# Seven products for the gate pair of layer two, with one of them run first, and a forget gate on column groups

## The chip, the cores and the metric

The kernel runs on one core of one Trainium2 chip. Times are device microseconds of one execution; the time of a version is the median of its runs. The engines meant below are TensorE (PE, and PEld for its weight loads), VectorE (DVE), ScalarE (ACT), GpSimd (POOL) and SyncE (SP), which here issues most DMAs.

## What is computed

Two layers of a streaming encoder, for 512 tokens of 2048 features, all in fp32. The parts that matter here:

```python
def hybrid_layer(x, w_in, w_out, g_pre, g_post, w_alpha, b_alpha, g_gla, g_att, rel_bias):
    h = rmsnorm(x, g_pre)
    z = h @ w_in
    gq, gk, gv, gg, ga, aq, ak, av, ag = split_columns(z)
    log_a = jax.nn.log_sigmoid((ga @ w_alpha + b_alpha).astype(jnp.float32)) / GLA_TAU
    o_gla = gla_chunk_causal(gq, gk, gv, log_a)
    ...
    o_gla = o_gla * jax.nn.silu(gg)
    o_att = chunk_band_attention(aq, ak, av, rel_bias)
    ...
    o_att = o_att * jax.nn.silu(ag)
    y = jnp.concatenate([o_gla, o_att], axis=-1) @ w_out
    return x + rmsnorm(y, g_post)
```

(Reshapes into heads are left out.) `ga`, the input of the forget gate, has only 16 columns. All else of `z` is 14 blocks of 512 columns: AG0 and AG1 (attention gate), AV0 and AV1, QK01 to QK67 (attention's queries and keys), GK and GQ, GV0 and GV1, GG0 and GG1. `w_out` is four more blocks, W01 and W23.

## The kernel before

**Products.** An fp32 product is made of three fp32r products: high times high, high times low, low times high, where the high part is a cast and the low part what the cast lost. Twelve matmuls of 128x512 (three terms, two halves of 256 input features, two token tiles) make a *job*: one block product for one of four chunks `c` of features. For the query and key blocks the result stands feature-major, and a job is 24 matmuls of 128x256.

A pair of blocks is multiplied for 512 tokens as a two-by-two scheme with seven block products P1 to P7 in place of eight (`fast_gemm`, L330): the input A is cut in token halves and feature halves (A11, A12, A21, A22), the weights in feature halves ("top", "bottom") and the two blocks. P1 uses A11 and P2 A12 directly, P4 uses A22, the others the sums S1 to S4 of the input, which `make_sums` (L554) writes to DRAM once for a layer. The right-hand factors are running sums of the four weight quarters in the tile H: P1 takes H itself, P5 and P6 add a quarter to it (L200), P7 subtracts (L202), P2 takes a raw quarter and then adds it to H (L222), after which P4 uses H. P3 uses the raw tile of P6. So a pair has 28 jobs, written in `PROD` as "10 11 50 12 ..." (product, chunk). Two accumulators X and Y of two PSUM banks each are used in turn; at the end of a product its result is copied out by ScalarE (L346) or combined by VectorE (L351) and handed to a consumer.

**Jobs and queues.** A job has a load (0.5 MB of weights by SP into a ring `raw` of five tiles or `H` of four, and the input's operand into `sa`, ring of four), a high part (ScalarE's cast into `wh`, four tiles, L206, with VectorE's running sum ahead of it) and a low part (VectorE into `wl`, three tiles, L216). While the matmuls of a job are issued, `ahead()` prepares loads five, high parts four and low parts three jobs ahead. Every engine's queue is served in order; the order on each is fixed when the program is built, by a scheduler that places instructions by estimated ready times. The rest (attention, the GLA recurrence, norms) are generator tasks, of which `pump` puts a few steps between jobs.

**The two layers.** Layer one multiplies AG0 and AG1 by a plain product (`std_gemm`, L299) while the input is prepared. Layer two does too, token half by token half, since the second half's tokens come later: 384 matmuls at L316. Then six pairs follow (`PAIRS`: AV, QKa, QKb, GK, GV, GG), then the out-projection (W01, W23) with an order of its own.

**The forget gate** (`forget_gate`, L751) multiplies the input's high and low parts by weights of 96 columns that hold the 16 gate columns split three times over in high and low parts: 64 matmuls of 128x256 a layer (L758), each keeping 96 of 128 columns of the array. `forget_gate_decay` (L773) multiplies its result, 98 rows, with `w_alpha` (L796, four matmuls a layer), all in fp32r.

**A22** is written to DRAM for P4 and loaded for each pair (`LEFT`, L185), 48 loads in all.

## Time and profile before

| what | us |
|---|---|
| median of 3 runs (lowest, highest) | 1615.64 (1615.36, 1617.37) |
| the profiled execution | 1613.77 |
| its span in the trace | 1611.8 |
| gate pair of layer two with its preparation (805.5 to 904.5) | 99.0 |
| six pairs of layer two (904.5 to 1448.3) | 543.8 |
| out-projection of layer two up to its last matmul (1448.3 to 1603.1) | 154.8 |

The stages' bounds are read from the first matmuls of each in the timeline. The profile is one execution; times in it count from the start of its span. "Busy" of TensorE overlaps, since a matmul's record lasts longer than the step to the next; steps are read from starts. An fp32 matmul appears as two records. A row of the groups names the line, the engine, the operation and the program's names, then busy time, mean duration and the idle time just before with what ended it. A row of the timeline has start, duration, and in brackets the idle time ahead. TensorE's granted clock is at full speed in all of the span. By stage, the columns being length, TensorE, its weight loads, VectorE, ScalarE and GpSimd, clock, DMA share and GB/s:

```profile
805.50:904.50 99.00, 98.85 (x483) 82.74 (x482) 80.63 (x109) 70.06 (x121) 21.61 (x40) 1.00 0.90 331
904.50:1448.30 543.80, 543.80 (x3293) 475.11 (x3292) 410.81 (x541) 297.01 (x503) 30.18 (x34) 1.00 0.75 259
1448.30:1603.10 154.80, 154.53 (x689) 127.27 (x687) 138.33 (x155) 90.08 (x132) 14.51 (x21) 1.00 0.78 268
```

### The profile page before, as it was taken

The numbers are of one execution on the slowest core, as the hardware profiler recorded it, in microseconds if no ns is written. First come the engines' busy times: TensorE is split into PE (matmuls) and PEld (weight loads), VectorE is DVE, ScalarE is ACT, GpSimd is POOL, SyncE is SP. The second block draws the span as 40 slices with busy tenths as digits, with TensorE's granted clock in tenths as the row PEclk, the third lists the DMA queues.
The fourth block names the chain that finished last, engine by engine and source line by source line (L and its number), as shares of the span: only waits on it lengthen the run. The fifth ranks groups of instructions, "written<-read, shape, count | busy, mean of one in ns | idle before, by whom it ended". The sixth has DMA issues, their size and how long they took to land.

```text
span 1611.8 us, 24496 instructions
## 1 busy us (share of the span) xinstructions
PE 1603.2 (99%) x8942; PEld 1373.1 (85%) x8942; DVE 1272.4 (79%) x1647; ACT 918.6 (57%) x1509; POOL 127.4 (8%) x192
## 2 busy tenths in 40 slices
PE   9999999999999999999999999999999999999998
PEld 7888999998888777888888889999988887788886
DVE  5977777678777877998988677786786778689887
ACT  7544445657455556665796444456675555465654
POOL 0120000010000000100122000000100000101001
PEclk9999999999999999999999999999999999999999
DMA  9797686685868768689779886867858687686887
GB/s 371 257 373 264 246 305 205 226 306 171 282 214 283 265 214 319 218 307 388 268 264 365 325 292 232 303 206 243 307 206 278 224 295 250 224 301 240 331 300 207
DMA packets 133928, 438.17 MB, mean 272 GB/s; under 512 B 14404, under 2 KB 27204, under 8 KB 133776
## 3 DMA queue, kind: packets, MB, share of 16 engines
q1 hardware_dynamic: 117360, 376.78, 66.9%
q0 software_dynamic: 16160, 59.53, 10.0%
q8 instruction: 71, 1.16, 0.3%
q14 instruction: 49, 0.40, 0.1%
q10 hardware_dynamic: 288, 0.30, 0.1%
HBM read 377.02 MB, written 61.62 MB: 272 GB/s over the span
## 4 chain that ended last, share of the span: by engine, by line
PE 95%; DVE 2%; DMA 1%; ACT 1%; issue 1%; SPq 0%; POOLq 0%; ACTq 0%; DVEq 0%
PE mm L394 54%; PE mm L384 19%; PE mm L316 10%; PE ax L951 2%; PE ax L394 2%; PE ax L1137 1%; PE ax L934 1%; PE ax L758 1%; PE ax L1109 1%; PE ax L914 1%; PE ax L913 1%; PE ax L912 1%; DVE wl L216 1%; DMA bias<-in_rel_dram 0%; PE ax L976 0%
## 5 line engine op out<-in xcount | busy, mean ns | idle before, releaser
L394 PE MATMUL mm<-wh,sa 128*128 128x512 f32 x1600 | 517.3, 394 | 0.5 <-ACT wh L206 0.5
L206 ACT CAST wh<-H 128x1024 fp32r<-128x1024 f32 x256 | 268.5, 1051 | 215.9 <-PE mm L394 96.1
L216 DVE TENSOR_TENSOR wl<-H,wh 128x1024 fp32r<-128x1024 f32 x256 | 311.9, 1220 | 93.3 <-PE mm L394 35.9
L394 PEld LDWEIGHTS mm<-wh,sa 128*128 128x128 f32 x1600 | 299.5, 188 | 72.3 <-issue 8.6
L206 ACT CAST wh<-raw 128x1024 fp32r<-128x1024 f32 (+1 forms) x233 | 243.9, 1051 | 204.4 <-PE mm L394 89.3
L216 DVE TENSOR_TENSOR wl<-raw,wh 128x1024 fp32r<-128x1024 f32 (+1 forms) x233 | 282.4, 1215 | 58.6 <-PE mm L394 23.5
L394 PE MATMUL mm<-wl,sa 128*128 128x512 f32 x800 | 312.7, 391 | 0.0
L384 PE MATMUL mm<-sa,wh 128*128 128x256 f32 x1280 | 237.4, 285 | 0.0
L394 PE MATMUL mm<-wh,a 128*128 128x512 f32 x640 | 211.5, 394 | 0.0
L384 PEld LDWEIGHTS mm<-sa,wh 128*128 128x128 f32 x1280 | 200.2, 191 | 0.3
L384 PE MATMUL mm<-sa,wl 128*128 128x256 f32 x640 | 181.0, 283 | 0.0
L394 PEld LDWEIGHTS mm<-wl,sa 128*128 128x128 f32 x800 | 150.3, 188 | 30.5 <-DVE wl L216 0.7
L200 DVE TENSOR_TENSOR H<-H,raw 128x1024 f32<-128x1024 f32 x144 | 174.8, 1218 | 1.0
L394 PEld LDWEIGHTS mm<-wh,a 128*128 128x128 f32 x640 | 119.5, 188 | 24.9
L394 PE MATMUL mm<-wl,a 128*128 128x512 f32 x320 | 125.7, 393 | 0.0
L384 PEld LDWEIGHTS mm<-sa,wl 128*128 128x128 f32 x640 | 122.5, 191 | 0.0
L436 POOL TENSOR_TENSOR sm<-sm,mhalf 128x2 f32<-128x2 f32 (+2 forms) x40 | 51.3, 1283 | 762.4 <-DVE sm L961 457.3
L202 DVE TENSOR_TENSOR raw<-H,raw 128x1024 f32<-128x1024 f32 x56 | 68.5, 1223 | 49.4 <-DMA raw<-in_w_dram 49.4
L394 PE MATMUL mm<-wh,g 128*128 128x512 f32 x320 | 101.5, 391 | 0.0
L384 PE MATMUL mm<-a,wh 128*128 128x256 f32 x512 | 95.4, 285 | 0.0
L346 ACT COPY ev<-mm 128x512 f32<-128x512 f32 x104 | 60.7, 584 | 60.0 <-PE mm L394 43.3
L222 DVE TENSOR_TENSOR H<-H,raw 128x1024 f32<-128x1024 f32 x48 | 58.7, 1223 | 38.0 <-DMA raw<-in_w_dram 37.7
(257 smaller groups left out, 2324.5 us busy)
## 6 DMA issues: line engine op xcount, KB each, us to landing
raw<-in_w_dram SPq DMA_DIRECT2D x311, 512.0 KB, 5.1
sa<-S SPq DMA_DIRECT2D x184, 512.0 KB, 4.5
H<-in_w_dram SPq DMA_DIRECT2D x64, 512.0 KB, 5.2
sa<-A SPq DMA_DIRECT2D x48, 512.0 KB, 6.2
S<-g POOLq DMA_DIRECT2D x32, 512.0 KB, 9.3
sa<-oS SPq DMA_DIRECT2D x32, 512.0 KB, 5.4
oS<-g POOLq DMA_DIRECT2D x16, 512.0 KB, 4.5
oS<-sa POOLq DMA_DIRECT2D x16, 512.0 KB, 5.7
```

Source lines behind the costliest of these rows:

```text
L200: nc.vector.tensor_tensor(out=h, in0=h, in1=r, op=ALU.add)
L202: nc.vector.tensor_tensor(out=r, in0=h, in1=r, op=ALU.subtract)
L206: last_cast[0] = nc.scalar.copy(self.wh[:, z, :], src[:, z, :]).ins
L216: last_low[0] = nc.vector.tensor_tensor(out=self.wl[:, z, :], in0=self.src[:, z, :], in1=self.wh[:, z, :].bitcast(F32), op=ALU.subtract).ins
L222: nc.vector.tensor_tensor(out=h, in0=h, in1=self.src, op=ALU.add)
L316: nc.tensor.matmul(pss[o], a(part, kk, o) if callable(a) else a[:, part, t], rhs[:, kk, :], start=(i == 0 and kk == 0 and m == 0), stop=(i ...
L346: last_copy[0] = nc.scalar.copy(e, src[t]).ins
L384: nc.tensor.matmul(dst, lhs[:, kk, f], a[:, part, tok], start=(fresh and kk == 0 and m == 0 and ft % 2 == 0), stop=(c == 3 and kk == 1 and ...
L394: last_mm[0] = nc.tensor.matmul(out_ps[t], a[:, part, tok], rhs[:, kk, :], start=(fresh and kk == 0 and m == 0), stop=(c == 3 and kk == 1 ...
L436: nc.gpsimd.tensor_tensor(out=out_r, in0=v, in1=mhalf[:, : v.shape[-1]], op=ALU.pow)
L758: nc.tensor.matmul(ps[0:96, half * 256 : (half + 1) * 256], wga[kt // 10][:, kt % 10, :], op[:, i, (kt % 2) * 256 : (kt % 2 + 1) * 256], s ...
L951: nc.tensor.matmul(o, self.pt[i][:, j * P : (j + 1) * P], av[hd // 4, j // 2][:, j % 2, (hd % 4) * P : (hd % 4 + 1) * P], start=(j == 0), ...
```

## The change

In layer two, AG becomes a pair of seven products like the others. `early_gemm` runs P2 (A12 times the first block's bottom quarter) of all seven pairs first, 28 jobs, as soon as the first token half is there; each result is copied out by ScalarE and written to DRAM by GpSimd's queue. The pairs then run `PROD_LATE`, 24 jobs. After P1 its copies get the early P2 added by two accumulating DMAs, and they are handed to the consumer after P4's job 1. With P2 gone from the pair, H lacks the bottom quarter, so P4 loads it again and adds it. P7's last job is ahead of P3's last; its combination is made at once, but in all pairs but AV its consumer runs only when P3 has ended. A22 is kept in four tiles for the layer. Layer one keeps `PROD`.

In both layers, the forget gate is computed by fp32 matmuls with 32 columns, on four column groups of the array by turns (the group `j` takes the feature block `2 kh + kk`), called once for each chunk inside `token_sums`, and the decay product is fp32 with 128 rows.

```diff
+    PROD_LATE = order("10 11 50 12 51 13 52 53 60 61 30 62 63 31 70 71 32 72 73 33 40 41 42 43")
...
-            elif k == "P2" or (k == "P4" and end):
+            elif k == "P2" or (k == "P4" and (end or late)):
                 p["r", self.c] = self.fetch(rtile("raw", bufs=5), b0, bottom)
...
+            if late and k == "P4":
+                if b0 == AG0:
+                    A[1, 1, c] = slot(f"a12{c}", [2, 512], F32R)
+                    nc.sync.dma_start(flat(A[1, 1, c]), src)
+                src = None
...
-                    if k in ("P5", "P6") or (k == "P4" and self.b0 >= NB_IN):
+                    if k in ("P5", "P6") or (k == "P4" and (self.b0 >= NB_IN or self.l)):
                         nc.vector.tensor_tensor(out=h, in0=h, in1=r, op=ALU.add)
...
-            stream += [Job(l, "std", c, b) for half in range(2) for b in (AG0, AG1) for c in CO]
+            stream += [Job(l, "std", 4 + c, b0) for b0, _ in (AG,) + PAIRS for c in range(4)]
...
+    def early_gemm(l, pair, rate):
+        acc = [ps_mm.tile([P, W], F32, tag="mm", name=nm("mm")) for _ in range(2)]
+        pace = Pace(rate)
+        for c in range(4):
+            job = take(l, pair[0], "std", 4 + c)
+            until(lambda: (1, 0, c) in A)
+            product(job, A[1, 0, c], acc, range(2), c == 0, c == 3, pair[0] in (QK01, QK45))
+            ahead()
+            pace()
+        for t in range(2):
+            e = ev()
+            last_copy[0] = nc.scalar.copy(e, acc[t]).ins
+            nc.gpsimd.dma_start(p2_d[pair][:, t, :], e)
...
-                consume(1, 1, t, None, combine(keep["p5"][t], src, ALU.subtract, keep["p5"][t]))
+                comb = combine(keep["p5"][t], src, ALU.subtract, keep["p5"][t])
+                if late and not direct:
+                    z = comb()
+                    held.append(lambda dst=None: z)
+                else:
+                    consume(1, 1, t, None, comb)
...
+            if late and (k, c) == ("P4", 1):
+                for t in range(2):
+                    finished("P2", t)
...
+                    if late:
+                        for t in range(2):
+                            nc.gpsimd.dma_start(keep["p1"][t], p2_d[pair][:, t, :], accum_op=ALU.add)
...
+                    if k == "P3":
+                        for t, comb in enumerate(held):
+                            consume(1, 1, t, None, comb)
...
+        def forget_gate(c):
+            if c == 0:
+                gate_ps.append(aux())
+            first = None
+            for half in (1, 0):
+                for j in (3, 2, 1, 0):
+                    kh, kk = divmod(j, 2)
+                    with tc.issue_after(first) if first else nullcontext():
+                        mm = nc.tensor.matmul(
+                            gate_ps[0][32 * j : 32 * (j + 1), half * 256 : (half + 1) * 256],
+                            fg_weights[l][:, 8 * kh + 2 * c + kk, :],
+                            full[half, c][:, kh, kk * 256 : (kk + 1) * 256],
+                            start=(c == 0 and half == 1), stop=(c == 3), skip_group_check=True,
+                        ).ins
...
         if l:
-            for half in range(2):
-                for q, b in enumerate((AG0, AG1)):
-                    std_gemm(
-                        l, b, (2 * half, 2 * half + 1), CO, operand_in, gate_evac(q), rate=1.3, lag=2 * half * q,
-                    )
-                if half == 0:
-                    tasks.append(token_sums(l))
-                    tasks.append(forget_gate())
+            tasks.append(token_sums(l, forget_gate))
+            for pair in (AG,) + PAIRS:
+                early_gemm(l, pair, 2.6)
+            fast_gemm(l, AG, gate_consume, rate=2.6)
...
-        fast_gemm(l, PAIRS[0], av_consume)
+        fast_gemm(l, PAIRS[0], av_consume, direct=True)
```

The function `product` holds the matmuls that stood in `fast_gemm` (L384, L394). Lines of the changed kernel differ: L200, L202 and L216 of before are L210, L212 and L226, L351 is L401, L316 is L326, L384 and L394 are L349 and L358.

The order of instructions changes with it. First VectorE in the pair AV of layer two, from the last subtraction for P7 on. Before (`L222` is P2's sum into H):

```order
L202 TENSOR_TENSOR raw_1795_9248<-H_1734_8951,raw_1795_9248 128x1024
L216 TENSOR_TENSOR wl_1788_9221<-raw_1766_9102,wh_1785_9203 128x1024
L202 TENSOR_TENSOR raw_1799_9269<-H_1744_8982,raw_1799_9269 128x1024
L216 TENSOR_TENSOR wl_1793_9244<-raw_1786_9205,wh_1789_9224 128x1024
L222 TENSOR_TENSOR H_1723_8879<-H_1723_8879,raw_1803_9290 128x1024
L216 TENSOR_TENSOR wl_1797_9264<-raw_1770_9123,wh_1794_9246 128x1024
L222 TENSOR_TENSOR H_1726_8897<-H_1726_8897,raw_1806_9308 128x1024
L216 TENSOR_TENSOR wl_1801_9285<-raw_1795_9248,wh_1798_9267 128x1024
L216 TENSOR_TENSOR wl_1804_9304<-raw_1799_9269,wh_1802_9288 128x1024
L351 TENSOR_TENSOR g0_1810_9329<-mm_1740_8963,ev_1791_9228 128x512
L222 TENSOR_TENSOR H_1734_8951<-H_1734_8951,raw_1813_9349 128x1024
L216 TENSOR_TENSOR wl_1807_9322<-raw_1803_9290,wh_1805_9306 128x1024
```

After (`L210` is now P4's sum into H; the last row is the low part of P4's job 0, the row two above it that of P3's job 3):

```order
L212 TENSOR_TENSOR raw_1886_9693<-H_1825_9393,raw_1886_9693 128x1024
L226 TENSOR_TENSOR wl_1884_9689<-raw_1879_9654,wh_1882_9673 128x1024
L212 TENSOR_TENSOR raw_1892_9718<-H_1838_9443,raw_1892_9718 128x1024
L226 TENSOR_TENSOR wl_1890_9713<-raw_1862_9569,wh_1885_9691 128x1024
L210 TENSOR_TENSOR H_1809_9316<-H_1809_9316,raw_1899_9757 128x1024
L226 TENSOR_TENSOR wl_1894_9734<-raw_1886_9693,wh_1891_9716 128x1024
L226 TENSOR_TENSOR wl_1897_9753<-raw_1892_9718,wh_1895_9737 128x1024
L210 TENSOR_TENSOR H_1816_9348<-H_1816_9348,raw_1902_9776 128x1024
L210 TENSOR_TENSOR H_1825_9393<-H_1825_9393,raw_1905_9795 128x1024
L226 TENSOR_TENSOR wl_1900_9771<-raw_1866_9590,wh_1898_9755 128x1024
L210 TENSOR_TENSOR H_1838_9443<-H_1838_9443,raw_1908_9814 128x1024
L226 TENSOR_TENSOR wl_1903_9790<-H_1809_9316,wh_1901_9774 128x1024
```

P4's four sums into H stand within seven rows, between the low parts of 32 and 40; before, the sums were P2's, and had more low parts between them.

Next VectorE at the end of the pair GG of layer two. Before (`L106` are the low halves of splits and `L1201` products of the combined results, the last row is the low part of the out-projection's first job):

```order
L106 TENSOR_TENSOR g15_2786_14255<-g12_2768_14160,g15_2786_14255 128x512
L216 TENSOR_TENSOR wl_2793_14305<-raw_2784_14248,wh_2788_14274 128x1024
L106 TENSOR_TENSOR g4_2791_14283<-g10_2767_14157,g4_2791_14283 128x512
L216 TENSOR_TENSOR wl_2800_14344<-H_2619_13531,wh_2794_14308 128x1024
L106 TENSOR_TENSOR g5_2797_14317<-g13_2769_14161,g5_2797_14317 128x512
L1201 TENSOR_TENSOR g10_2767_14157<-g10_2767_14157 128x512
L1201 TENSOR_TENSOR g13_2769_14161<-g13_2769_14161 128x512
L216 TENSOR_TENSOR wl_2804_14367<-H_2638_13599,wh_2801_14346 128x1024
L106 TENSOR_TENSOR g0_2792_14289<-g10_2767_14157,g0_2792_14289 128x512
L351 TENSOR_TENSOR ev_2674_13757<-mm_2632_13578,ev_2674_13757 128x512
L106 TENSOR_TENSOR g1_2798_14323<-g13_2769_14161,g1_2798_14323 128x512
L216 TENSOR_TENSOR wl_2807_14385<-H_2802_14348,wh_2805_14369 128x1024
```

After (`L109` and `L1227` are the same lines, `L1339` sums of another task; the row of `H_2809_14212` is the first job's low part):

```order
L226 TENSOR_TENSOR wl_2818_14252<-H_2666_13578,wh_2808_14210 128x1024
L1339 TENSOR_TENSOR bias_2747_13922<-bias_2747_13922,t2_2840_14336 128x256
L1339 TENSOR_TENSOR sg_2784_14079<-sg_2784_14079,t2_2840_14336 128x256
L1339 TENSOR_TENSOR bias_2747_13922<-bias_2747_13922,t2_2841_14340 128x256
L1339 TENSOR_TENSOR sg_2784_14079<-sg_2784_14079,t2_2841_14340 128x256
L226 TENSOR_TENSOR wl_2821_14270<-H_2809_14212,wh_2819_14254 128x1024
L226 TENSOR_TENSOR wl_2844_14366<-raw_2820_14256,wh_2822_14272 128x1024
L109 TENSOR_TENSOR g14_2825_14281<-g9_2810_14214,g14_2825_14281 128x512
L109 TENSOR_TENSOR g4_2827_14291<-g10_2811_14215,g4_2827_14291 128x512
L1227 TENSOR_TENSOR g10_2811_14215<-g10_2811_14215 128x512
```

The splits of the combined results, ahead of the out-projection's first low part before, now come behind it, and four quarter rows of L1339 stand ahead.

Last TensorE at the forget gate. Before, in layer one, between the plain product's matmuls:

```order
L316 MATMUL mm_105_622<-wh_130_750,a122_121_692 128x512
L758 MATMUL ax_162_952<-a112_115_669,g16_132_754 96x256 x4
L758 MATMUL ax_162_952<-a113_124_710,g16_132_754 96x256 x4
L758 MATMUL ax_162_952<-a120_75_429,g16_132_754 96x256 x4
L758 MATMUL ax_162_952<-a121_112_651,g17_133_755 96x256 x4
L316 MATMUL mm_106_623<-wh_130_750,sa_122_703 128x512
L316 MATMUL mm_106_623<-wl_139_810,sa_122_703 128x512
L316 MATMUL mm_106_623<-wh_130_750,sa_122_703 128x512 x2
L316 MATMUL mm_106_623<-wl_139_810,sa_122_703 128x512
L316 MATMUL mm_106_623<-wh_130_750,sa_122_703 128x512
L758 MATMUL ax_162_952<-a122_121_692,g17_133_755 96x256 x4
```

After, in layer two, inside the early product of a feature-major pair (`L349`):

```order
L349 MATMUL mm_1631_8287<-a122_1542_7871,wh_1614_8218 128x256 x2
L787 MATMUL ax_1635_8318<-g14_1603_8153,g16_1627_8278 32x256 x4
L787 MATMUL ax_1635_8318<-H_1529_7834,g16_1627_8278 32x256 x4
L787 MATMUL ax_1635_8318<-g15_1610_8190,g16_1627_8278 32x256 x4
L787 MATMUL ax_1635_8318<-H_1538_7857,g16_1627_8278 32x256 x4
L349 MATMUL mm_1631_8287<-a122_1542_7871,wl_1620_8253 128x256
L349 MATMUL mm_1631_8287<-a122_1542_7871,wh_1614_8218 128x256 x2
L349 MATMUL mm_1631_8287<-a122_1542_7871,wl_1620_8253 128x256
```

A row of four matmuls is one token half of one chunk, one matmul for each column group; the four rows are the calls for two chunks.

More of the change, by code (lines that the diff above doesn't have):

```diff
@@ L161, in load @@
             end = b0 >= NB_IN and k != "std"
+            late = self.l and b0 < NB_IN
             if end:
@@ L328, in hybrid_trunk, with product @@
     roles = ["XY", "YX"]
-    def fast_gemm(l, pair, consume, rate=0.0, skip=0, feature_major=False, after=None, end=False, lag=0, ops=A):
-        b0 = pair[0]
+    def product(job, a, out_ps, ts, fresh, final, feature_major, apart=False):
+        for kk, some in [(kk, (t,)) for t in ts for kk in range(2)] if apart else [(kk, ts) for kk in range(2)]:
+            if feature_major:
+                for ft in range(4):
+                    f = slice(ft * P, (ft + 1) * P)
+                    tok = slice(kk * 256, (kk + 1) * 256)
+                    dst = out_ps[ft // 2][:, (ft % 2) * 256 : (ft % 2 + 1) * 256]
+                    terms = ((job.wh, 0), (job.wh, 1), (job.wl, 0))
+                    for m, (lhs, part) in enumerate(terms):
+                        nc.tensor.matmul(
+                            dst, lhs[:, kk, f], a[:, part, tok],
+                            start=(fresh and kk == 0 and m == 0 and ft % 2 == 0),
+                            stop=(final and kk == 1 and m == 2), skip_group_check=True,
+                        )
+            else:
+                for t in some:
+                    tok = slice(kk * 256 + t * P, kk * 256 + (t + 1) * P)
+                    terms = ((0, job.wh), (0, job.wl), (1, job.wh))
+                    for m, (part, rhs) in enumerate(terms):
+                        last_mm[0] = nc.tensor.matmul(
+                            out_ps[t], a[:, part, tok], rhs[:, kk, :],
+                            start=(fresh and kk == 0 and m == 0),
+                            stop=(final and kk == 1 and m == 2), skip_group_check=True,
+                        ).ins
@@ L332, in fast_gemm @@
+    def fast_gemm(l, pair, consume, rate=0.0, skip=0, feature_major=False, after=None, end=False, lag=0, ops=A, direct=False):
+        b0, held = pair[0], []
         acc = {n: [ps_mm.tile([P, W], F32, tag="mm", name=nm("mm")) for _ in range(2)] for n in roles[0]}
@@ L552, in prep_half, with make_sums @@
             yield
-    def make_sums(dst, tags, parts, home={}, chunks=range(4)):
+    def make_sums(dst, tags, parts, home, before):
         stage = [0]
@@ L587, in make_sums, with token_sums, parts @@
             yield
-    def token_sums(l):
-        return make_sums(sa_d[l], STAGE, lambda c: (full[0, c][:, 0, :], full[0, c][:, 1, :], full[1, c][:, 0, :], full[1, c][:, 1, :]), HOME)
+    def token_sums(l, before):
+        def parts(c):
+            return tuple(full[half, c][:, kh, :] for half in range(2) for kh in range(2))
+        return make_sums(sa_d[l], STAGE, parts, HOME, before)
     VT = ("g16", "g17", "g4", "g5", "g6", "g7", "g12", "g13")
```

145 lines of the change are left out of this document (52 added, 93 removed).

## The prediction

> **What bounds the kernel now.** I read the page first, then the chain of waits, then the groups by line, and last the timeline and the windows of the stages that the change touches.
>
> ```profile
> span 1611.8 us, 24496 instructions
> PE 1603.2 (99%) x8942; PEld 1373.1 (85%) x8942; DVE 1272.4 (79%) x1647; ACT 918.6 (57%) x1509; POOL 127.4 (8%) x192
> PE 95%; DVE 2%; DMA 1%; ACT 1%; issue 1%; SPq 0%; POOLq 0%; ACTq 0%; DVEq 0%
> ```
>
> TensorE is busy for 1603.2 of 1611.8 us and carries 95% of the chain that ended last. So a matmul that goes is worth its full step, unless the weight parts for the next one then come too late. The profiled execution took 1613.77 us, 1.87 us under the median of 1615.64 us; all terms below are differences against that execution, and the sum is put on the median. A measurement of this kernel can tell some 0.2%, 3.2 us, from no change.
>
> What comes next after TensorE is seen in two places. The first is the loop of weight loads inside a pair of layer two (SP's rows are the DMA issues, from the timeline of 1008 to 1036 us):
>
> ```profile
> SPq L156 <- DVE wl L216: 44.9, 27, 3.7
> DVE raw L202 <- DMA raw<-in_w_dram: 10.0, 8, 2.0
> raw<-in_w_dram SPq DMA_DIRECT2D x311, 512.0 KB, 5.1
> 1019.90 1.22 DVE L216 TENSOR_TENSOR wl<-raw,wh 128x1024 fp32r<-128x1024 f32 x1
> 1021.15 0.33 SPq L156 DMA_DIRECT2D raw<-in_w_dram  x1
> 1026.83 1.23 DVE L222 TENSOR_TENSOR H<-H,raw 128x1024 f32<-128x1024 f32 x1 [2.20 <-DMA raw<-in_w_dram]
> 1027.98 1.22 DVE L216 TENSOR_TENSOR wl<-raw,wh 128x1024 fp32r<-128x1024 f32 x1
> ```
>
> The reader is to see a circle: a low part (L216) ends at 1021.12, SP at once issues the load for which that raw buffer had to come free, VectorE waits 2.20 us and starts the sum with it at 1026.83, 5.7 us after the low part's end. In the two query and key pairs (980 to 1172 us, the first two rows) SP waits 44.9 us in this way and VectorE 10.0 us for such loads. The second place is the out-projection of layer two:
>
> ```profile
> 1420.00:1440.00 20.00, 20.00 (x98) 16.50 (x97) 17.18 (x25) 14.03 (x23) 0.00 (x0) 1.00 0.93 340
> ...
> 1460.00:1480.00 20.00, 20.00 (x94) 16.62 (x93) 19.97 (x27) 13.72 (x21) 2.13 (x4) 1.00 0.49 171
> 1480.00:1500.00 20.00, 19.73 (x87) 15.81 (x86) 19.37 (x23) 13.53 (x22) 2.13 (x4) 1.00 0.73 252
> 1500.00:1520.00 20.00, 20.00 (x90) 16.56 (x89) 20.00 (x21) 10.08 (x14) 2.13 (x4) 1.00 0.99 372
> 1486.42 0.73 PE L394 MATMUL mm<-wh,sa 128*128 128x512 f32 x2 [0.27 <-ACT wh L206]
> PE mm L394 <- ACT wh L206: 0.5, 2, 0.3
> ```
>
> A window's busy times are TensorE, weight loads, VectorE, ScalarE and GpSimd in that order: VectorE works 59.3 of 60 us from 1460 to 1520. TensorE already runs dry there, by 0.27 us, and the last row (waits of TensorE over the whole span: total, times, longest) shows that its products wait for a weight part twice, 0.5 us in all. There VectorE and TensorE are equally long.
>
> **The change part by part.**
>
> *Seven products for the gate pair.* The pair AG now needs 336 matmuls of 128x512 in place of 384 (seven products of four jobs of twelve, against a plain product). That the products are spread over two places (28 jobs early, 24 in the pair) changes no count.
>
> ```profile
> 84.99 1.10 PE L758 MATMUL ax<-a,g 128*96 128x256 f32 x8
> 85.93 1.11 PE L758 MATMUL ax<-g,g 128*96 128x256 f32 x8
> 86.87 0.40 PE L316 MATMUL mm<-wh,sa 128*128 128x512 f32 x1
> 87.11 0.40 PE L316 MATMUL mm<-wl,sa 128*128 128x512 f32 x1
> 87.34 0.62 PE L316 MATMUL mm<-wh,sa 128*128 128x512 f32 x2
> 87.80 0.39 PE L316 MATMUL mm<-wl,sa 128*128 128x512 f32 x1
> 88.03 0.39 PE L316 MATMUL mm<-wh,sa 128*128 128x512 f32 x1
> 88.27 1.10 PE L758 MATMUL ax<-g,g 128*96 128x256 f32 x8
> ```
>
> Busy times overlap, so I go by starts: six matmuls from 86.87 to 88.27, 0.233 us each. 48 fewer are **-11.2 us**. A job of twelve is 2.8 us.
>
> *The forget gate.* Gone are 128 matmuls of 96 columns: sixteen from 84.99 to 86.87, 0.1175 us each, 15.0 us in both layers. The eight decay products change from one pass (L796) to fp32.
>
> ```profile
> L796 PE MATMUL ax<-g x8: 395/398/473, 372.5 to 1194.5; 98*128 98x512 f32 x8
> 372.46 0.40 PE L796 MATMUL ax<-g 98*128 98x512 f32 x1
> 372.69 0.40 PE L394 MATMUL mm<-wh,a 128*128 128x512 f32 x1
> L1370 PE MATMUL ax<-g,t x2: 592/644/697, 1605.6 to 1606.1; 128*128 128x512 f32 x2
> 538.28 0.39 PE L394 MATMUL mm<-wh,a 128*128 128x512 f32 x1
> 538.60 1.08 PE L1137 MATMUL ax<-g,g 128*64 128x256 f32 x8
> 539.61 0.50 PE L394 MATMUL mm<-wh,sa 128*128 128x512 f32 x1
> ```
>
> L796 took 0.23 us, 1.8 us for eight. An fp32 product shows as two records (L1370, one instruction), 0.5 us apart: eight products of 512 columns are 8.0 us. The new gate is eight calls of eight fp32 matmuls, 32 output columns each, sixteen records of 256 columns on four column groups. No row shows four groups; the nearest is L1137, eight fp32 records of 256 columns on two groups of 64: from 538.28 to 539.61 are 1.33 us, 1.10 without the 0.23 of the matmul ahead. One after another eight records of 0.25 (half of L1370's 0.5) would be 2.0, so the two groups run side by side, in four steps. If four groups do so as well, a call is four steps too, 1.10 us, eight calls 8.8. If only two do, eight steps, 2.0 us and 16 in all; if none, 16 records of 0.25, 4.0 us and 32. I take the first, since two distinct groups demonstrably overlap: 8.8 + 8.0 - 15.0 - 1.8 = **0.0 us**, with +7 and +23 as upper ends. The removed splits of gate weights (L758's operands) lie on ScalarE and VectorE, which stand beside TensorE.
>
> A rule speaks against this part: the Trainium skill, "TensorE: Matmul & The Clock Gate", section "Part 3: Packing small matmuls", says that weight loads overlap running matmuls only where the row group differs, and column groups share all rows. By it the third case would hold, and the sum would be 23 us higher; L1137's halves share their rows too and do run side by side, so the trace does not bear it out for two groups.
>
> *P2 early, P7 ahead of P3's end, P4 reloaded.* Work per layer changes little: VectorE's sum into H moves from P2 (L222) to P4 (L200), one for one, at the same 1.14 us; twelve weight loads, fourteen writes and fourteen accumulating reads of P2 come in, 24 reads of A22 go. Over the span 272 GB/s move, and the busiest quoted window carries 372, so I cost bytes at nothing; their cover is the early stage, where 28 jobs need one weight load each. The cost is order. Before, each P4 job had a P2 job between, so that four sums with a fresh raw buffer stood in front of seven jobs; now four jobs 40 41 42 43 follow 33 at once and each needs a sum. On VectorE such a sum waits ahead of the low parts of 33 and 40, and whoever waits for those is TensorE. The circle is 5.7 (low's end to sum) + 1.15 (sum, 1026.83 to 1027.98) + 1.15 (low) = 8.0 us, against a lead of at most three jobs, 8.4 us, where a low part is made three jobs ahead. Bounds for a pair: nothing where the lead is whole, and 8.0 - 2 x 2.8 = 2.4 us where one job of it is gone; over seven pairs 0 to 17 us. I take 0.6 a pair, **+4 us**, near the lower end: before, the same circle with its 2.20 us wait runs in the same pairs, and of the 0.5 us that products wait for weights in the whole span at most 0.23 can be its doing.
>
> *P7's results held until P3's end.* In the last pair of the stage (GG) this pushes multiplications behind the first low part of the out-projection. By the instruction order eight halves of 512 columns (the six splits and two products with g's) that stood ahead of W01's first low part stand behind it, and four quarter rows of 256 columns have come ahead.
>
> ```profile
> 1445.50 0.68 DVE L351 TENSOR_TENSOR ev<-mm,ev 128x512 f32<-128x512 f32 x1
> 1446.10 0.68 DVE L1201 TENSOR_TENSOR g<-g,g 128x512 f32<-128x512 f32 x1
> 1446.70 0.42 DVE L1313 TENSOR_TENSOR bias<-bias,t 128x256 f32<-128x256 f32 x1
> 1447.03 0.42 DVE L1313 TENSOR_TENSOR sg<-sg,t 128x256 f32<-128x256 f32 x1
> ```
>
> A half is 0.60 us from start to start and a quarter 0.33: 8 x 0.60 - 4 x 0.33 = 3.5 us more for VectorE in the stretch where it is 59.3 of 60 us busy. Bounds: nothing, if GG's idle time (2.8 us in 1420 to 1440) lets the first low parts run earlier, and 6 us if ScalarE's halves of these splits come late as well. I take **+3.5 us**; only the 0.27 us gap shows that there is no reserve.
>
> *The boundary of the layers* (other transposes' order, gate inside the token sums) I cost at +0.3 us: the gate is issued where its operands have just been written, one short wait a call hidden by the early products; without that cover it is one transposition's copy, some 1 us.
>
> Sum: -11.2 + 0.0 + 4 + 3.5 + 0.3 = **-3.4 us**: 1610.4 us for an execution like the profiled one, **1612.2 us** on the median.
>
> **The rivals.**
>
> *The stalls do not come* (0.22). VectorE's lead absorbs the new order, and the matmul count alone rules. For it: VectorE is 79% busy, and in layer two it has four fewer low parts. Against it: the full windows above. Time: 1615.64 - 11.2 + 0.3 = 1604.7 us, with 1602 as the lower end if a gate call costs a little less than reckoned.
>
> *The loop of loads decides, slower* (0.20). Place: the four sums before P4 in all seven pairs of layer two; price 2.4 us each, 17 us. It decides from (11.2 + 3.2 - 3.8) / 7 = 1.5 us a pair upward. For it: SP's 44.9 us. Against it: no TensorE gap there now. Time: 1615.64 - 11.2 + 17 + 3.8 = 1625.2; with two thirds of the price 1619.6.
>
> *Only two column groups at a time* (0.12): 1612.2 + 7 = 1619.2 us. *One at a time*, the skill's rule as told above, worked from the 0.25 us records (0.04): 1635 us.
>
> *The change does not do what it says*: the 48 matmuls are gone in the instruction stream, so only their place in time could fail, by an early stage that waits for operands A12 at the layers' boundary (0.02): each chunk late by a transposition's 1 us, 1616.
>
> **How the numbers follow.** The forecast has 0.40. Its own range is 1608 to 1617, the late pairs between 0 and 8 us. Chances: faster by over 0.2% (below 1612.4) is half of the forecast, all of the first rival and a little of the rest, 0.44; slower (above 1618.9) most of the second rival's upper part, most of the two column cases, 0.26; within 0.2% the rest, 0.30. The range 1602 to 1623 takes in the first rival, the case of two groups and the lower half of the loop's; out are its full price and the single groups, under 0.2.
>
> **What would show it.** Gate pair: 336 matmuls in it and the early part at 0.23 us. Forget gate: a call of sixteen records from the matmul ahead to the next in 1.3 us; 2.2 or 4 speak for the rivals. Late pairs: VectorE idle ahead of L210's sums (now with P4), releaser a raw load, and TensorE idle before low parts (L226) of 33 and 40 to 43, 0.6 us a pair; 2.4 is the loop, none is the first rival. Out-projection: TensorE idle of some 3.5 us in its first half with VectorE full. I would be wrong if any new wait stood elsewhere: before accumulated P2 copies are read behind P4,1, or at the layers' boundary.

## The result and the profile after

The changed kernel took 1629.83 us (median of five runs, 1624.07 to 1630.90), the kernel before 1615.38 us (five runs). The ratio is 1.0079 with an interval of 1.0063 to 1.0094: slower by 0.8%, where 1612.2 us had been forecast and 1623 was the upper end of the range. The profiled execution took 1630.84 us, 17.07 us more than the one of before.

The page and the waits of TensorE (total, times, longest) of the changed kernel, and its windows by stage (length, then busy time of TensorE, weight loads, VectorE, ScalarE and GpSimd, granted clock, DMA share, GB/s), here the last early product, AG, AV, GV and W01; the sum line is over the stages of layer two up to the start of W23:

```profile
PE 1605.4 (99%) x8902; PEld 1357.7 (83%) x8902; DVE 1272.1 (78%) x1629; ACT 918.4 (56%) x1509; POOL 142.0 (9%) x218
PE 89%; DMA 6%; DVE 2%; issue 1%; ACT 1%; SPq 0%; POOLq 0%; ACTq 0%; DVEq 0%
PE mm L359 <- DMA sa<-S: 7.1, 8, 2.7
PE mm L359 <- ACT wh L216: 3.9, 6, 1.6
PE mm L359 <- DVE wl L226: 3.8, 6, 1.0
882.80:892.30 9.50, 9.13 (x40) 6.89 (x38) 4.14 (x4) 5.27 (x8) 2.15 (x4) 1.00 1.03 421
892.30:965.40 73.10, 70.44 (x298) 56.79 (x299) 50.44 (x46) 32.97 (x39) 6.16 (x10) 0.98 0.91 341
965.40:1036.70 71.30, 67.49 (x290) 53.53 (x290) 50.32 (x46) 31.34 (x37) 2.83 (x4) 1.00 0.89 311
...
1285.80:1373.10 87.30, 83.13 (x423) 68.11 (x421) 67.12 (x93) 46.31 (x86) 7.38 (x9) 0.98 0.72 247
...
1463.40:1544.30 80.90, 78.92 (x352) 63.97 (x351) 77.69 (x92) 51.44 (x79) 8.61 (x16) 1.00 0.77 280
sum 736.10, PE 721.72 PEld 611.82 DVE 568.75 ACT 415.83 POOL 75.25; mean PE 48.11 PEld 40.79 DVE 37.92 ACT 27.72 POOL 5.02
```

Before, products waited 0.5 us for weight parts; now 7.7 us for their two parts and 7.1 us straight for a DMA, the load of the input's sums, and DMA is 6% of the chain that ended last, not 1%. TensorE stands idle for 736.10 - 721.72 = 14.4 us in layer two up to W23: 2.7 in AG, 3.8 in AV, 4.2 in GV, 2.0 in W01. The same stretch took 721.6 us before, so it holds 14.5 of the profile's 17 us. The other 2.6 lie ahead of it: the first matmul of layer two starts at 808.2 us, before at 805.5. In the runs below that have the same layer one it starts at 806.0 to 807.9; apart from a wait at the layers' boundary (0.63 us, before 0.17) this part was not looked into.

Busy time understates the loss, since a matmul's record outlasts its step. From starts: before, the 4800 matmuls of 128x512 took 1110.8 us, 0.2314 each; now 4752 of them take 1128.7. At the old step they would take 1099.7, so the lower count is worth 11.1 us, and longer steps took 29.0 us. The trace shows where they come from. These are pieces of the chain that ended last (start, length), and TensorE's row at 1354 us, with the loads that SP issued ahead of it:

```profile
874.77 15.37 DMA raw<-in_w_dram
956.78 16.09 DMA H<-in_w_dram
1344.24 10.12 DMA sa<-S
...
1342.68 1.47 SPq L160 DMA_DIRECT2D raw<-in_w_dram  x2
1344.24 0.49 SPq L195 DMA_DIRECT2D sa<-S  x1
1344.95 2.13 SPq L160 DMA_DIRECT2D raw<-in_w_dram  x2
...
1354.50 0.47 PE L359 MATMUL mm<-wh,sa 128*128 128x512 f32 x1 [2.69 <-DMA sa<-S]
```

A load that took 5 us at the median takes 10 to 16 us at the end of the early products and of pairs. In GV, SP issues five loads of 0.5 MB between 1342.68 and 1347.08 us; the operand issued among them at 1344.24 lands ten microseconds later, and TensorE waits 2.69 us for it. The mean rate of the pair does not show it: GV moves 247 GB/s now and moved 260 before, when TensorE did not wait. What is full is a stretch of 16 us in it (first GV before, then this stretch):

```profile
1269.40:1355.60 86.20, 86.20 (x420) 69.19 (x419) 70.63 (x88) 44.87 (x67) 5.43 (x6) 1.00 0.75 260
...
1346.00:1362.00 16.00, 11.83 (x44) 9.02 (x44) 12.34 (x15) 5.53 (x7) 0.54 (x1) 0.89 1.01 396
```

At the end of the early products and the start of AG, 64 us in a row are full. Here is that stretch with its transfers, and behind the dots the end of the gate pair before, with its weight loads from 851 to 905 us:

```profile
848.00:912.00 64.00, 62.79 (x336) 52.28 (x328) 44.44 (x51) 33.45 (x46) 15.39 (x29) 1.00 1.02 406
raw<-in_w_dram SPq DMA_DIRECT2D x17, 512.0 KB, 12.0
S<-g POOLq DMA_DIRECT2D x16, 512.0 KB, 12.6
p<-ev POOLq DMA_DIRECT2D x10, 256.0 KB, 9.9
...
876.30:904.50 28.20, 28.20 (x151) 24.18 (x150) 19.14 (x22) 13.04 (x17) 5.04 (x10) 1.00 1.03 412
raw<-in_w_dram SPq DMA_DIRECT2D x17, 512.0 KB, 9.5
```

There P2's results (`p`) are written in the same stretch as the 16 sums of the input, and weight loads take 12.0 us at the median. Before, 28 us at 412 GB/s with loads of 9.5 us did not make TensorE wait: full engines make loads late, and it depends on the lead whether TensorE feels it.

Not all of AG's idle time is a late load's. Its longest wait, the 1.62 us up to 912.77, is for a high part:

```profile
906.92 1.23 DVE L210 TENSOR_TENSOR H<-H,raw 128x1024 f32<-128x1024 f32 x1 [0.77 <-DMA raw<-in_w_dram]
910.51 1.26 ACT L396 COPY ev<-mm 128x512 f32<-128x512 f32 x2 [5.62 <-PE mm L359]
911.67 1.05 ACT L216 CAST wh<-H 128x1024 fp32r<-128x1024 f32 x1
```

The sum that this cast reads had ended at 908.15, and ScalarE stood idle. But the two copies of P1's result stand ahead of the cast in its queue, and they have to wait for TensorE to end P1. So this wait comes from the order on ScalarE; the low part behind the cast adds 0.52 us.

### The profile page after: what moved, and what is told of

Same layout as the page of the kernel before. It is cut to its first block, busy times and chain, and to the rows that moved or that the text cites. A ratio compares the mean times of both kernels' runs of the same rounds, so it can differ in the third digit from the quotient of the medians.

```text
span 1629.0 us, 24464 instructions
## 1 busy us (share of the span) xinstructions
PE 1605.4 (99%) x8902; PEld 1357.7 (83%) x8902; DVE 1272.1 (78%) x1629; ACT 918.4 (56%) x1509; POOL 142.0 (9%) x218
## 2 busy tenths in 40 slices
DMA packets 138828, 451.62 MB, mean 277 GB/s; under 512 B 15026, under 2 KB 27570, under 8 KB 138676
## 4 chain that ended last, share of the span: by engine, by line
PE 89%; DMA 6%; DVE 2%; issue 1%; ACT 1%; SPq 0%; POOLq 0%; ACTq 0%; DVEq 0%
PE mm L359 52%; PE mm L349 19%; PE mm L326 5%; DMA raw<-in_w_dram 3%; DMA sa<-S 2%; PE ax L977 2%; PE ax L359 2%; DVE wl L226 1%; PE ax L960 1%; PE ax L1163 1%; DMA H<-in_w_dram 1%; PE ax L1135 1%; PE ax L940 1%; PE ax L939 1%; PE ax L938 1%
## 5 line engine op out<-in xcount | busy, mean ns | idle before, releaser
L216 ACT CAST wh<-H 128x1024 fp32r<-128x1024 f32 x272 | 284.8, 1052 | 260.2 <-PE mm L359 96.9
L226 DVE TENSOR_TENSOR wl<-H,wh 128x1024 fp32r<-128x1024 f32 x272 | 330.7, 1219 | 91.9 <-ACT wh L216 34.8
L216 ACT CAST wh<-raw 128x1024 fp32r<-128x1024 f32 (+1 forms) x213 | 223.0, 1051 | 178.9 <-PE mm L359 75.7
L226 DVE TENSOR_TENSOR wl<-raw,wh 128x1024 fp32r<-128x1024 f32 (+1 forms) x213 | 257.9, 1214 | 61.0 <-PE mm L359 29.7
L359 PE MATMUL mm<-wh,a 128*128 128x512 f32 x864 | 283.2, 396 | 1.7 <-ACT wh L216 1.6
L210 DVE TENSOR_TENSOR H<-H,raw 128x1024 f32<-128x1024 f32 x180 | 218.4, 1218 | 25.5 <-DMA raw<-in_w_dram 24.8
L349 PE MATMUL mm<-sa,wh 128*128 128x256 f32 x1152 | 213.4, 285 | 0.5 <-DMA sa<-S 0.5
L359 PEld LDWEIGHTS mm<-wh,a 128*128 128x128 f32 x864 | 161.1, 188 | 37.8 <-ACT wh L216 3.0
L349 PEld LDWEIGHTS mm<-sa,wh 128*128 128x128 f32 x1152 | 179.8, 192 | 0.8 <-issue 0.6
L359 PE MATMUL mm<-wl,a 128*128 128x512 f32 x432 | 169.9, 393 | 0.2 <-DVE wl L226 0.2
L349 PE MATMUL mm<-sa,wl 128*128 128x256 f32 x576 | 162.8, 283 | 0.0
L349 PE MATMUL mm<-a,wh 128*128 128x256 f32 x640 | 119.8, 286 | 0.0
L212 DVE TENSOR_TENSOR raw<-H,raw 128x1024 f32<-128x1024 f32 x60 | 73.3, 1222 | 53.8 <-DMA raw<-in_w_dram 53.8
L349 PEld LDWEIGHTS mm<-sa,wl 128*128 128x128 f32 x576 | 110.2, 191 | 0.0
L349 PEld LDWEIGHTS mm<-a,wh 128*128 128x128 f32 x640 | 100.1, 191 | 1.4 <-issue 0.8
L359 PEld LDWEIGHTS mm<-wl,a 128*128 128x128 f32 x432 | 81.2, 188 | 18.7 <-issue 1.3
```

Source lines behind the costliest of these rows:

```text
L210: nc.vector.tensor_tensor(out=h, in0=h, in1=r, op=ALU.add)
L212: nc.vector.tensor_tensor(out=r, in0=h, in1=r, op=ALU.subtract)
L216: last_cast[0] = nc.scalar.copy(self.wh[:, z, :], src[:, z, :]).ins
L226: last_low[0] = nc.vector.tensor_tensor(out=self.wl[:, z, :], in0=self.src[:, z, :], in1=self.wh[:, z, :].bitcast(F32), op=ALU.subtract).ins
L349: nc.tensor.matmul(dst, lhs[:, kk, f], a[:, part, tok], start=(fresh and kk == 0 and m == 0 and ft % 2 == 0), stop=(final and kk == 1 and ...
L359: last_mm[0] = nc.tensor.matmul(out_ps[t], a[:, part, tok], rhs[:, kk, :], start=(fresh and kk == 0 and m == 0), stop=(final and kk == 1 a ...
```

## The experiments

Each was timed beside the kernel before (1614.4 to 1615.4 us). I give medians, and stalls as idle time in the windows view.

**The gate alone.** Before, with the new gate and decay product and nothing else.

> The kernel of before with the new forget gate alone (both layers, fp32 decay product too). Theory G: in the profile of the changed kernel a call of sixteen records takes 1.31 us from the matmul ahead to the next, all eight 8.4 us after the first matmul of each, and the fp32 decay products 3.6 us, against 15.1 and 2.0 before, so 5 us fall: about 1611 us. Rival: what falls there only lets TensorE wait elsewhere for weights or for the token sums: 1615 us as before.

1615.82 us, ratio 1.0004 (0.9995 to 1.0014): no change. The calls are as short as in the changed kernel, where one of them looks like this:

```profile
65.19 0.40 PE L326 MATMUL mm<-wh,a 128*128 128x512 f32 x1
65.51 0.64 PE L787 MATMUL ax<-g,g 128*32 128x256 f32 x8
65.97 0.61 PE L787 MATMUL ax<-H,g 128*32 128x256 f32 x8
66.52 0.50 PE L326 MATMUL mm<-wh,a 128*128 128x512 f32 x1
```

From 65.19, the matmul ahead, to 66.52, the next one, are 1.33 us for sixteen records, so four column groups do run side by side. What comes back stands at the decay product, here in the run with the gate alone:

```profile
371.21 1.02 PE L782 MATMUL ax<-g 128*128 128x512 f32 x2
371.67 0.80 PE L394 MATMUL mm<-wh,a 128*128 128x512 f32 x1
372.30 0.40 PE L394 MATMUL mm<-wl,a 128*128 128x512 f32 x1
```

From 371.21 to 372.30 are 1.09 us, 0.86 without the 0.23 of the matmul between: the step behind the fp32 product is longer as well, 6.9 us for eight. So the gate part is worth nothing that can be measured, as forecast. Theory G had counted the decay products' records alone, 3.6 us for these 6.9, which is 3.3 of its 5 us.

**Without P2's transfers.**

```diff
-            nc.gpsimd.dma_start(p2_d[pair][:, t, :], e)
...
-                            nc.gpsimd.dma_start(keep["p1"][t], p2_d[pair][:, t, :], accum_op=ALU.add)
```

> The changed kernel without the fourteen writes of the early P2 and the fourteen accumulating reads (P2's part is missing from the result). Theory T (too many bytes at once: the stretch from 855 to 912 us moves 418 GB/s without a break, and loads take up to 16 us): the 12 us of TensorE's stalls in the pairs AG and AV shrink to a third, time about 1621 us. Theory S (P4's reloads block SP's queue, operand loads queue behind them): nothing changes in GV and GG and little elsewhere, 1626 to 1630 us.

1621.60 us, 8 less. AG's idle time falls from 2.7 to 1.9 us, GV's from 4.2 to 2.2; AV's stays at 3.9. So 7 MB cost 8 us, but not only where theory T had put them. And not all of it is bytes: without the writes, the program's order on ScalarE is another, with the cast that the first job after P1 needs ahead of P1's copies:

```profile
903.32 1.05 ACT L216 CAST wh<-H 128x1024 fp32r<-128x1024 f32 x1 [4.37 <-DVE H L210]
908.04 1.27 ACT L395 COPY ev<-mm 128x512 f32<-128x512 f32 x2 [3.67 <-PE mm L359]
```

AG's wait of 1.62 us is gone here and in the run without either part below; in all other runs of the changed kernel it stands before the same matmul.

**Without P4's reload, and its two halves apart.** First without load and sum; then the load alone; then the sum alone (the tile added to itself).

```diff
-            elif k == "P2" or (k == "P4" and (end or late)):
+            elif k == "P2" or (k == "P4" and end):
...
-                    if k in ("P5", "P6") or (k == "P4" and (self.b0 >= NB_IN or self.l)):
+                    if k in ("P5", "P6") or (k == "P4" and self.b0 >= NB_IN):
```

> The changed kernel without the reload of a weight quarter for P4 in layer two and without its sum (P4 of layer two then lacks that quarter). 28 loads and 28 VectorE sums fewer. Theory S: stalls of GV, GG and the out-projection (some 11 us) go and those of AV in part, about 1615 us. Theory T: the stretch of AG stays full, since the reloads come only at the pairs' ends, and 1624 us or more remain.

> The changed kernel with P4's reload kept and its sum on VectorE left out (P4 of layer two lacks a quarter). Without reload and sum the kernel was 17 us faster. Theory B (the 14 MB of reloads are too much beside the other transfers): some 15 of the 17 us stay, about 1627 us. Theory R (the reload holds one of the five raw buffers until its sum has had its turn on VectorE, so SP stands and all loads behind it come late): the buffer is free as soon as the load has landed, some 12 us go, about 1616 us.

> The changed kernel with P4's reload left out and its sum kept, which adds the tile to itself (P4 of layer two is wrong by that). Theory V (the 28 sums of 1.14 us stand in VectorE's way): about 1627 us. Theories B and R, where the load or its buffer matters: within 3 us of the kernel without both, 1613 to 1615 us.

1612.67, 1627.50 and 1612.27 us. Without the load 17 us go; the 28 sums on VectorE cost nothing that can be measured, and a load whose sum is gone costs as much as before. So nothing hangs on the sum's turn in VectorE's queue. AV and GV with the sum and without the load:

```profile
964.10:1029.40 65.30, 65.30 (x289) 54.08 (x289) 50.14 (x44) 31.64 (x36) 2.83 (x4) 1.00 0.86 297
...
1279.30:1358.80 79.50, 79.50 (x413) 66.68 (x412) 66.84 (x91) 46.25 (x85) 7.74 (x9) 1.00 0.72 251
```

**The operand's load first**, ahead of the weight load of the same job.

> The changed kernel with the input operand's load issued ahead of the weight load of the same job in layer two's pairs. Theory S in its narrow form (the operand load stands behind a weight load that waits for a raw buffer; TensorE waits 7.6 us for operand loads in all): these 7.6 us go, about 1621 us. Rival (the transfers themselves are late, whoever is first): the waits only change places, 1626 to 1631 us.

1625.08 us, interval of the ratio 1.0042 to 1.0076, which overlaps the changed kernel's: a small gain at most. In its profiled execution, the slowest of its four, AV and GG lost stalls and QKa and the last early product got some.

**Own buffers.** P4's quarters go to the four tiles of A22, and A22 is loaded for each pair again (24 loads more); in the second run no A22 is loaded, and P4 multiplies A11.

```diff
+            elif k == "P4" and late:
+                p["r", self.c] = self.fetch(slot(f"a12{self.c}", [2, 512]), b0, bottom)
```

> The changed kernel with P4's quarters loaded into the four tiles that hold A22 (no raw buffer is used), and A22 loaded again for each pair, as before the change: 24 loads, 12 MB more. Theory R: the stalls of AV, GV and GG go, about 1617 us. Theory B: more bytes, 1630 us or more.

> The changed kernel with P4's quarters in four tiles of their own (those of A22) and no bytes more: P4 of layer two multiplies A11 in place of A22, so its product is wrong. Against the changed kernel only the raw buffers are freed of P4's loads (and four loads of A22 in AG are gone). Theory R (the ring of five raw buffers, with 16 loads in 24 jobs): most of the 17 us that the reload costs go, 1613 to 1618 us. Theory B (the transfers themselves): 1624 us or more.

1627.39 and 1619.49 us. Own buffers take away 10 of the 17 us (with four loads of A22 fewer than in the changed kernel). The first run has 28 loads of A22 that the second has not, and is 8 us slower; TensorE waits 6.1 us for them there. AV of the second:

```profile
964.70:1030.00 65.30, 65.30 (x290) 54.09 (x289) 50.66 (x45) 33.64 (x38) 2.83 (x4) 1.00 0.94 343
```

AV moves 343 GB/s here and TensorE is never idle; in the changed kernel it was idle for 3.8 us at 311. So the rate of bytes by itself does not stall that pair.

**The sum by an accumulating DMA**, behind P7's subtraction.

```diff
+                            nc.gpsimd.dma_start(h, quarter, accum_op=ALU.add)
```

> The changed kernel with P4's quarter added to H by an accumulating DMA on GpSimd's queue, right behind P7's subtraction for the same chunk: same bytes from DRAM, no raw buffer, no sum on VectorE. Theory R: about 1614 us, near the kernel without reload. Theory B: the bytes are the same, 1625 us or more; slower also if such a transfer takes longer than the six jobs (16 us) between P7 and P4 of a chunk.

1650.53 us, the slowest of the changed kernel's variants: TensorE waits 20.9 us for operand loads. No raw buffer and no sum on VectorE, and yet 21 us worse. Whether it is the accumulating, GpSimd's queue or the earlier place was not looked into.

**More transfers in the kernel before.** Four or eight copies of 0.5 MB from DRAM to DRAM in each pair of layer two, which nobody reads.

> The kernel of before with four more transfers of 0.5 MB in each of layer two's six pairs, at P4's jobs: a copy of a weight quarter from DRAM to DRAM that nobody reads, so no buffer, no sum and no order is touched but SP's queue, which issues it. Theory B (the load on the DMA engines): before had 40 loads in 76 us of a pair, now 44, 301 MB per ms, about what the changed kernel has (36 loads and P2's two transfers in 66 us, 296): AV, GV and GG get stalls, 1620 to 1628 us. Rival (what hurts is the closer order of the 24 jobs, with its operands needed sooner): 1615 to 1617 us.

> The same with eight more transfers in each pair, at P3's and P4's jobs, 329 MB per ms. Theory B: clearly more than with four, 1630 us or more. Rival: 1615 to 1618 us.

1634.12 and 1663.13 us, but these two do not say what they were made for: nothing tied the copies to their place, and they were issued in layer one from 62 us on, beside the writing of the first sums. Of the run with four:

```profile
80.00:100.00 20.00, 20.00 (x120) 17.66 (x119) 10.17 (x17) 4.58 (x8) 4.87 (x9) 1.00 1.02 420
100.00:120.00 20.00, 15.93 (x61) 11.87 (x61) 14.47 (x16) 10.63 (x14) 3.76 (x7) 0.91 1.03 419
120.00:140.00 20.00, 10.49 (x37) 7.87 (x36) 9.24 (x10) 5.76 (x7) 0.54 (x1) 0.74 0.57 226
```

They show what full DMA engines do when it lasts: at first TensorE is not idle at 420 GB/s, and then it is, for 4.1 and 9.5 of 20 us. Then with the copies tied to SP's load ahead of them, and the same in the changed kernel without P4's reload, so that it has its bytes back and no buffer and no job that waits for them (the copies write DRAM too, which the loads did not):

```diff
+                with tc.issue_after(last_load[0]):
+                    last_load[0] = nc.sync.dma_start(spare, w[self.l, b0, bottom].rearrange("p (k n) -> p k n", k=2)).ins
```

> Again the kernel of before with 24 more transfers of 0.5 MB, now tied to the load ahead of them in SP's queue, so that they stand in layer two's six pairs, four at P4's jobs of each (in the run without the tie they were issued in layer one from 62 us on). Theory B: layer two's pairs get stalls of 5 to 20 us in sum, 1620 to 1635 us. Rival (before's pairs have the reserve, and what hurts is the closer order of 24 jobs): within 2 us of before.

> The changed kernel without P4's reload and sum, and with as many transfers of the same quarters from DRAM to DRAM at the same place of SP's queue: the bytes of the changed kernel, but no buffer that fills and no job that waits for them. Theory B: back at 1624 to 1630 us. Theory R (a job has to wait for its load, or a buffer for its job): 1612 to 1617 us, as 24 such transfers cost the kernel of before only 3 us.

1617.82 us (ratio 1.0017, 1.0008 to 1.0026), some 3 us more than before, and 1622.95 us, 10 more than without the reload. AV of the first and of the second:

```profile
904.40:981.90 77.50, 76.47 (x338) 63.03 (x337) 55.72 (x51) 35.07 (x38) 0.62 (x2) 1.00 0.82 309
966.10:1033.90 67.80, 67.27 (x289) 55.15 (x290) 44.98 (x41) 31.43 (x36) 2.82 (x4) 0.97 0.90 314
```

So pairs of 28 jobs bear 24 more transfers for 3 us, pairs of 24 jobs pay 10 for 28. The mean rate does not tell them apart: AV of the first is idle for 1.0 us at 309 GB/s, that of the changed kernel for 3.8 at 311.

**P7 without its load**, its subtraction kept.

> The changed kernel with P4's reload and sum kept and P7's weight load left out in layer two's pairs (its subtraction stays and takes H twice, so P7's product is wrong). 28 loads fewer, as without P4's reload, but at another place of the pair. Theory B: the same 15 to 17 us go, 1612 to 1615 us. Rival (the place counts: loads at the pair's end, behind which the next pair's stand): 1624 us or more.

1618.63 us: 11 less than the changed kernel, where theory B had 15 to 17 and its rival at most 6. So loads count at this place too. That they count for less than P4's can come from the place, or from the raw buffers: P7 still takes its four of the ring, which the run without P4's reload frees. No run tells the two apart. AV still has 1.5 us of idle time.

**Neither P2's transfers nor P4's reload.**

> The changed kernel without P4's reload and sum and without P2's writes and accumulating reads (both parts missing from the result). Theory B: both gains add, 17 + 8 us from 1630, about 1605 us, which is the matmul count alone (48 fewer, 11 us) with the 3.5 us of the out-projection on top. Rival (the two take the same stalls away): 1611 us.

1607.76 us, ratio 0.9963 (0.9949 to 0.9976). The two gains, 8 and 17, add to 22. What is left above the pure count is in AG and W01.

**GG's P7 not held**, alone and with the operand's load first.

```diff
-        fast_gemm(l, PAIRS[5], gg_consume, rate=3, after=fetch_operands)
+        fast_gemm(l, PAIRS[5], gg_consume, rate=3, after=fetch_operands, direct=True)
```

> The changed kernel with P7's results of the pair GG handed on at P7's end, not held until P3's end. The step of the prediction: the out-projection's stall (2.5 us more than before by the profile) goes, 2.5 us faster than the changed kernel. Rival: the stall there has another cause (VectorE's work is the same in sum), and the time stays within 1 us.

> The changed kernel with both repairs that leave the result as it is: the operand's load ahead of the weight load, and GG's P7 not held. Each alone gained about 5 us. Theory B: bytes are the same, so the gains do not add fully: about 1621 us, still slower than before. Rival (the queue's order was the larger part): 1616 us or less.

1623.84 and 1626.09 us. By what steps take beyond 0.227 us, W01 of layer two loses 1.1 us before the change, 3.7 after, 2.5 with this edit: holding is worth 1.1 of the 2.6 us. The rest of the 6 us gained lies in AV and GV and is no more than the changed kernel's own runs differ, 1624 to 1631. The two edits together gain no more than one. Both versions compute the whole result and stay slower than before; of such versions I found none that beats it.

## Why the prediction was wrong

- **Gate pair, -11.2 us:** right. 48 matmuls fewer are 11.1 us at the step of before. The run with neither P2's transfers nor P4's reload bears it out: it is 7.0 us faster than before, and idle for 2.3 us in AG and 2.0 in W01.
- **Forget gate, 0.0 us:** right in the sum and in its parts. A call takes 1.33 us, four column groups at once, and the eight decay products 6.9 us for the 8.0 reckoned. Alone it changed the time by a ratio of 1.0004. The rule of the Trainium skill ("TensorE: Matmul & The Clock Gate", section "Part 3: Packing small matmuls") that weight loads overlap only where row groups differ, read as the prediction read it, would have made it 23 us more; these calls do not bear it out.
- **Late pairs, +4 us: this step failed.** The 4 us were the price of VectorE's sums ahead of the low parts, and those sums cost nothing that can be measured. What cost was the term put at nothing: "so I cost bytes at nothing", since 272 GB/s on the mean are less than 372 in a busy window, with the early stage as cover. P2's transfers cost 8 us, a part of it through the order on ScalarE, and P4's loads 17, both together 22. The stage that was to be the cover already moved 412 GB/s at its end before. The count was short too: the rows have sixteen weight loads more (`raw` 311 to 323, `H` 64 to 68) and sixteen loads of the input's sums more (184 to 200), where the prediction had twelve and none, and twenty reads of A22 fewer, not 24. With P2's transfers 13.5 MB came in (451.62 for 438.17); the prediction's list makes about 1. And a pair has lost four of its 28 jobs and its four reads of A22, but none of its 20 weight loads, which now come in bunches at the pairs' ends. There a load takes 10 to 16 us, as long as the lead of three to five jobs (8.4 to 14 us) or longer.
- **The loop of loads** was the rival of the right sign, price 17 us, with 0.20. Its place was right in AV and GV, its mechanism only in part: it made TensorE wait for sums on VectorE, which cost nothing, while the waits are for operands and weight parts behind late loads. So it is luck that its 17 us are the 17 that P4's loads cost. Raw buffers do matter: freed of P4's loads they give back 10 of 17 us.
- **Held results, +3.5 us in W01:** 2.6 measured, of which 1.1 go when GG's result is handed on at once. The sign was right, the size too large by a third, and the cause by more; what makes up the other 1.5 us was not looked into.
- **The boundary of the layers, +0.3 us:** right. The wait of the transposes there for ScalarE grew from 0.17 to 0.63 us. The early products behind it are idle for 0.4 us, all in the last.

What stays open: bytes and buffers are not two separate shares. The same bytes without buffers or waiting jobs cost 10 of the 17 us, own buffers at the same bytes save 10, and 28 other loads fewer with the buffers kept save 11; both together make the full price. That a load which meets full engines and a full ring is late for both is the reading that fits them; it is argued, not shown by a run of its own. AG is idle for 1.9 us or more in every run of the changed kernel. Where P2's results are written, the order on ScalarE is 2.1 us of it; no run kept them and changed that order, and none took the sums' writes away.

## What to carry to other kernels

A change that takes matmuls out of a stage bound by TensorE leaves less time for all that feeds the rest: count the transfers per job and per stage before and after, with those that the change itself adds, and look at the time from issue to landing and at the fullest ten or twenty microseconds, not at mean GB/s. Ask of each load how long its buffer is held and which loads stand behind it in the same queue, and of each cast what stands ahead of it on its engine. Tie an added test transfer to its neighbours, or the scheduler moves it.

## What was not expected of the hardware

After a stall TensorE's granted clock can drop to half. Two windows of the changed kernel, and TensorE's rows around them:

```profile
914.00:915.00 1.00, 0.97 (x4) 0.79 (x5) 1.00 (x1) 0.00 (x0) 0.00 (x0) 0.82 1.04 414
915.00:916.00 1.00, 1.00 (x4) 0.81 (x3) 0.11 (x1) 0.80 (x1) 0.00 (x0) 0.50 1.08 297
...
912.77 0.73 PE L359 MATMUL mm<-wh,g 128*128 128x512 f32 x2 [1.62 <-ACT wh L216]
914.03 0.50 PE L359 MATMUL mm<-wl,g 128*128 128x512 f32 x1 [0.52 <-DVE wl L226]
...
914.98 1.05 PE L359 MATMUL mm<-wh,g 128*128 128x512 f32 x2
915.83 0.63 PE L359 MATMUL mm<-wl,g 128*128 128x512 f32 x1
916.26 1.05 PE L359 MATMUL mm<-wh,g 128*128 128x512 f32 x2
```

After two stalls of 1.62 and 0.52 us the clock stands at 0.50 and a step takes 0.427 us (three from 914.98 to 916.26), up to about 918; the same follows the 2.69 us at 1354. Each time this costs some 1.6 us more (eight steps of 0.427 in place of 0.227). But it does not always come. In the run with own buffers at the same bytes, the same two waits, 1.62 and 0.53 us, left the clock of the whole pair AG at 1.00:

```profile
891.90:964.70 72.80, 69.49 (x299) 55.48 (x300) 52.15 (x47) 32.43 (x40) 6.17 (x10) 1.00 0.91 343
912.45 0.73 PE L358 MATMUL mm<-wh,g 128*128 128x512 f32 x2 [1.62 <-ACT wh L215]
```

What decides it, these runs do not show. The changed kernel's five runs fit: the two of 1624 us had a mean clock of 0.998 and 0.999, the three of 1630 us 0.996 to 0.997. The Trainium skill ("TensorE: Matmul & The Clock Gate", section "Part 1: The HAM clock gate (the "warmup" mystery)") has such a step down to half for windows of some 3.4 us, after a window that was idle; the length agrees with the rows, but here 2.1 us of idle time within 3.3 us were enough, in one run and not in the other.
